# Sums and differences of the Fourier weights made earlier, by VectorE through DRAM, and two squares more per stream left to the matmul

## The chip, the cores and the metric

The kernel runs on one core of one Trainium2 chip. The metric is the device time of one execution in microseconds (us), as the median of several runs. A difference within 0.2% is one that a measurement of this kernel can hardly tell from none.

## What is computed

A block of two layers works on 256 latent tokens and 256 context tokens of 1024 features. Each layer is a half SwiGLU FFN, a token mixer and a second half SwiGLU FFN; each of the three is preceded by an RMS norm with a shift and a scale, and added to the stream through a gate. Layer 0 mixes by a two-dimensional Fourier transform in four groups of 256 features, followed by a weight matrix; layer 1 mixes by retention. Cut to what matters:

```python
def half_ffn(t, m, j):
    h = modulate(rmsnorm(t, norm_g[l, j]), m[3 * j], m[3 * j + 1])
    return t + 0.5 * m[3 * j + 2] * swiglu(h, w_gate, w_up, w_down)

def fourier_mix(h):                       # layer 0
    hg = h.reshape(b, n, 4, 256)
    f = jnp.fft.fft2(hg, axes=(1, 3), norm="ortho").real
    return f.reshape(b, n, d)

def fourier_layer(h_lat, h_ctx, w, bias):
    return fourier_mix(h_lat) @ w + bias, fourier_mix(h_ctx) @ w + bias
```

Everything is float32. The kernel makes one float32 product of three TensorE matmuls: each operand is split into a rounded part ("hi") and the rest ("lo"), and hi x hi, hi x lo and lo x hi are added up.

## The kernel before, in words

The streams lie transposed, features on partitions, as eight tiles of 128 features by 256 tokens for each of the two streams (xlat, xctx). Weights come from DRAM in blocks of 1 MB by the SP queue into three buffers (`raw`, `rpool`), are split by ScalarE (`wh`, line 88, a cast) and VectorE (`wl`, line 89, a subtraction) into a ring of five buffers for each of the two parts (`wpool`, 1024 columns each), and are read by TensorE (`mm3`, lines 126 to 128). The order in which each engine's instructions stand is set by a scheduler that simulates the program; `tc.issue_after` holds an instruction back behind another.

The first FFN walks over 22 blocks of gate and up weights in three chunks (`half_ffn`, loop over i), each chunk followed by four blocks of the down projection (b). Beside it VectorE makes the modulation vectors by row products (`ada_step`, line 216, called by `pump`), whose weights POOL loads (line 207). The last chunk's down projection ends in `project_last`: for each of the eight tiles d and both streams s VectorE adds the residual (line 363), `scale_parts` makes the scaled hi and lo parts that the Fourier stage reads (lines 341 and 342), and `square` squares the tile (ScalarE, line 265) and adds the square to the running sum (POOL, line 272). With `apart=True` the square of the last tile, d = 7, is not added but kept as a second tile in `sums[s]`, and the matmul that sums over features adds it (`start` and `stop` over the list).

The Fourier stage (`fourier`) goes thus:

- `wide_tails` (lines 485 to 488) splits the weights of four lone frequencies and the bias.
- `stage1` transforms along features, for three (stream, group) pairs ahead; then `rstd_tokens` (line 352) makes the sums over features of the squares, one column for each half stream, and from them the reciprocal root (lines 357 and 359).
- For each pair `fold` (lines 587 to 591) applies the root and adds and subtracts halves, splits the result (`t` of line 89), and `stage2` transforms along tokens. In the trace these tiles are the `t` of the matmuls ps<-a,t.
- Then the weight matrix: four blocks b of two output tiles, each a product over odd and even frequencies, with residual (line 363), square and add (line 272; stream 0 on VectorE, stream 1 on POOL). Block 0 is loaded in `project_last` ahead of its last block (`fourier_weights`), blocks 1 to 3 inside the stage.

The weights of a frequency and of its mirror are needed as sum and difference. `load_folded` loads both matrices of a block (two loads of 1 MB) and POOL adds and subtracts them in place (line 107, two instructions of 128 x 1024 a block), so four blocks take eight loads in the three `raw` buffers and eight POOL instructions. After the last block `prepare(0, 2, T2)` makes the norm for the second FFN (lines 300 to 316 for the latent stream), whose first two weight blocks are split by POOL (`begin_two`, line 89 on POOL).

## Time and profile before

| | us |
|---|---|
| median of 3 runs (1679.35 to 1683.1) | 1680.78 |
| the profiled execution | 1683.79 |
| its span, first to last instruction | 1682.0 |
| TensorE busy in the span | 1637.4 (97%) |
| VectorE busy | 1142.1 (68%) |
| ScalarE busy | 627.6 (37%) |
| POOL busy | 174.9 (10%) |

The span is cut by the stages: the start to about 50 us, the first FFN to 397 us, the Fourier stage to about 463 us, and then the second, third and fourth FFN with the retention layer before the last. All times in the text are from the start of the span. A time behind a matmul in the timelines is its modelled duration; the distance between two starts says what it costs. The clock column gives the granted TensorE clock: 1.00 is 2.4 GHz, 0.50 is 1.2 GHz, and a value between them is a stretch with some time at either.

### The profile page before, as it was taken

What the parts mean: (1) busy time and instruction counts of PE and PEld (TensorE: products, weight loads), DVE (VectorE), ACT (ScalarE), POOL (GpSimd) and SP (SyncE); (2) the same over time, 40 slices, a digit from 0 to 9 for tenths busy, and PEclk for the clock granted to TensorE, in tenths of its full rate; (3) what the DMA queues carried; (4) which work ended last, traced back from release to release, by engine and by line L of the source; (5) the groups of instructions that cost most, each with busy time, mean ns of one, the idle gap of its engine ahead of it and who ended that gap; (6) DMA issues with size and microseconds to landing.
All of it is one profiled execution on the core that took longest, in us unless ns stands there. A gap on an engine that the chain in (4) does not pass through costs nothing.

```text
span 1682.0 us, 23132 instructions
## 1 busy us (share of the span) xinstructions
PE 1637.4 (97%) x9320; PEld 1431.1 (85%) x9320; DVE 1142.1 (68%) x1760; ACT 627.6 (37%) x913; POOL 174.9 (10%) x211
## 2 busy tenths in 40 slices
PE   6999999998899999999999999999999999999998
PEld 4788888887898888888888888888998989999998
DVE  5678788777966766766566776743677757575554
ACT  4422322244552223233342222233464454454444
POOL 0010011035310000000400000000400000110000
PEclk9999999999899999999999999999999999999999
DMA  9555555543324444444334444522233324345452
GB/s 328 211 189 200 194 178 217 191 170 138 120 87 155 168 172 163 177 170 166 116 121 166 161 166 160 188 95 92 77 124 126 126 101 150 128 166 180 167 195 70
DMA packets 53403, 263.63 MB, mean 157 GB/s; under 512 B 6832, under 2 KB 8240, under 8 KB 35120
## 3 DMA queue, kind: packets, MB, share of 16 engines
q1 hardware_dynamic: 34176, 193.47, 32.4%
q0 software_dynamic: 18576, 68.17, 11.7%
q8 instruction: 73, 1.20, 0.3%
q10 hardware_dynamic: 544, 0.52, 0.1%
q14 instruction: 34, 0.28, 0.1%
HBM read 261.08 MB, written 1.05 MB: 156 GB/s over the span
## 4 chain that ended last, share of the span: by engine, by line
PE 88%; DVE 6%; DMA 2%; ACT 1%; issue 1%; POOL 1%; SPq 0%; DVEq 0%; POOLq 0%; ACTq 0%
PE ps L127 29%; PE ps L128 29%; PE ps L126 29%; DMA raw<-in_wgu 1%; DVE wl L89 1%; DVE q L330 1%; DVE h L332 1%; ACT wh L88 1%; DMA a<-in_ada_first 1%; DVE xctx L363 1%; DVE xlat L363 1%; DMA q<-q 0%; PE ps L818 0%; DMA xctx<-in_x 0%; PE aux L244 0%
## 5 line engine op out<-in xcount | busy, mean ns | idle before, releaser
L88 ACT CAST wh<-raw 128x1024 fp32r<-128x1024 f32 x344 | 352.9, 1030 | 710.3 <-PE ps L127 659.7
L127 PE MATMUL ps<-h,wh 128*128 128x512 f32 (+1 forms) x1600 | 563.7, 354 | 5.2 <-DVE h L332 5.1
L128 PE MATMUL ps<-h,wl 128*128 128x512 f32 (+1 forms) x1600 | 562.2, 354 | 0.0
L126 PE MATMUL ps<-h,wh 128*128 128x512 f32 (+1 forms) x1600 | 556.9, 355 | 3.2 <-ACT h L88 2.2
L89 DVE TENSOR_TENSOR wl<-raw,wh 128x1024 fp32r<-128x1024 f32 x328 | 392.7, 1200 | 168.0 <-ACT wh L88 158.6
L127 PEld LDWEIGHTS ps<-h,wh 128*128 128x128 f32 x1600 | 303.0, 190 | 48.1 <-DVE h L332 6.6
L126 PEld LDWEIGHTS ps<-h,wh 128*128 128x128 f32 x1600 | 299.5, 190 | 45.8 <-ACT h L88 3.0
L128 PEld LDWEIGHTS ps<-h,wl 128*128 128x128 f32 x1600 | 303.0, 190 | 41.2
L216 DVE CUSTOM_DVE_ANT_0 dump<-araw,wide,adab 128x1024 bf16<-128x1024 f32 x256 | 329.6, 1288 | 4.3 <-DMA araw<-in_ada_w 0.5
L128 PE MATMUL ps<-a,wl 128*128 128x512 f32 (+2 forms) x952 | 320.1, 338 | 2.5 <-DVE wl L89 2.5
L127 PE MATMUL ps<-a,wh 128*128 128x512 f32 (+2 forms) x952 | 320.3, 338 | 0.0
L126 PE MATMUL ps<-a,wh 128*128 128x512 f32 (+2 forms) x952 | 318.8, 338 | 0.2 <-ACT wh L88 0.2
L128 PEld LDWEIGHTS ps<-a,wl 128*128 128x128 f32 x952 | 182.3, 192 | 21.4 <-DVE wl L89 2.9
L127 PEld LDWEIGHTS ps<-a,wh 128*128 128x128 f32 x952 | 182.3, 192 | 18.6
L126 PEld LDWEIGHTS ps<-a,wh 128*128 128x128 f32 x952 | 181.4, 192 | 19.0 <-ACT wh L88 0.4
L430 DVE TENSOR_TENSOR t<-ps,t 128x512 f32<-128x512 f32 (+1 forms) x88 | 55.0, 625 | 188.4 <-PE ps L128 181.1
L207 POOL DMA_DIRECT2D araw<-in_ada_w x128 | 67.7, 529 | 811.3 <-DVE mods L216 742.9
L363 DVE SCALAR_TENSOR_TENSOR xlat<-ps,mods,xlat 128x256 f32<-128x256 f32 x128 | 61.1, 481 | 63.8 <-PE ps L128 63.1
L428 ACT ACTIVATE t<-ps 128x512 f32<-128x512 f32 (+1 forms) x88 | 47.9, 544 | 133.6 <-PE ps L128 133.6
L89 DVE TENSOR_TENSOR a<-t,a 128x512 fp32r<-128x512 f32 (+2 forms) x116 | 71.1, 617 | 3.9 <-ACT a L88 3.6
L89 POOL TENSOR_TENSOR wl<-raw,wh 128x1024 fp32r<-128x1024 f32 x16 | 40.0, 2516 | 282.9 <-ACT wh L88 281.0
L88 ACT CAST a<-t 128x512 fp32r<-128x512 f32 (+2 forms) x116 | 64.2, 557 | 9.2 <-DVE t L847 7.4
(208 smaller groups left out, 1201.8 us busy)
## 6 DMA issues: line engine op xcount, KB each, us to landing
raw<-in_wgu SPq DMA_DIRECT2D x85, 1024.0 KB, 4.9
araw<-in_ada_w POOLq DMA_DIRECT2D x128, 512.0 KB, 3.7
raw<-in_wd SPq DMA_DIRECT2D x32, 896.0 KB, 5.5
raw<-in_ret_in SPq DMA_DIRECT2D x24, 1024.0 KB, 4.8
raw<-in_wd SPq DMA_DIRECT2D x16, 1024.0 KB, 6.7
a<-in_ada_first SPq DMA_DIRECT2D x32, 256.0 KB, 5.1
raw<-in_four_w SPq DMA_DIRECT2D x8, 1024.0 KB, 4.9
raw<-in_ret_out SPq DMA_DIRECT2D x8, 1024.0 KB, 4.7
```

Source lines behind the costliest of these rows:

```text
L88: mark[6] = nc.scalar.copy(hi, src)
L89: i = (lo_eng or nc.vector).tensor_tensor(lo, src, f32(hi), ALU.subtract)
L126: nc.tensor.matmul(ps, lh, rh, start=start, stop=False)
L127: nc.tensor.matmul(ps, lh, rl, start=False, stop=False)
L128: mark[4] = nc.tensor.matmul(ps, ll, rh, start=False, stop=stop)
L207: nc.gpsimd.dma_start(raw, a["ada_w"][l, m, d])
L216: nc.vector.tensor_tensor_reduce(dump, raw, wide[:, v, :], 1.0, adab[:, l, m, d : d + 1], ALU.mult, ALU.add, mods[l][:, m, d, v : v + 1],)
L330: nc.vector.scalar_tensor_tensor(u, x_tile(d, s), sc, r, ALU.mult, ALU.mult)
L332: done.append(nc.vector.scalar_tensor_tensor(lo, u, sh, f32(hi), ALU.add, ALU.subtract))
L363: mark[0] = nc.vector.scalar_tensor_tensor(x_tile(d, s), ps, mods[l][:, m, d, s : s + 1], x_tile(d, s), ALU.mult, ALU.add)
L428: mark[1] = nc.scalar.activation(sg[:, :width], psg[:, :width], AF.Silu)
L430: nc.vector.tensor_tensor(hf[:, :width], psu[:, :width], sg[:, :width], ALU.mult)
```

## The change

- `load_folded` is gone. `fold_step` loads a quarter of the two matrices' pair (two loads of 512 KB, 128 x 1024), VectorE adds and subtracts in place (two instructions of 128 x 512), and SP stores the result in a DRAM tile `folded`. There are eight such steps, one after every second gate and up block of the first FFN (i odd, from 3 to 17), each held behind the block's last split. Its buffers take 12 KB of a partition; the space for the DMA descriptors of the POOL queue is cut to 4 KB for them (last line of the diff).
- The four Fourier weight blocks are then single loads of 1 MB from `folded`, split as any other block.
- `wide_tails` is called with block 0, ahead of the last down projection block.
- `square(apart=...)` takes a count. At the end of the first FFN it is 2: the squares of d = 6 and d = 7 are left to the matmul of `rstd_tokens`, which has three parts instead of two. Elsewhere it is 0 or 1 as before.

```diff
+    fpool = ctx.enter_context(tc.tile_pool(name="fpool", bufs=1))
+    dpool = ctx.enter_context(tc.tile_pool(name="dpool", bufs=1, space=bass.MemoryType.DRAM))
...
-    def load_folded(src, other, n):
-
-        raw, two = load_raw(src, n), load_raw(other, n)
+    folded = dpool.tile([4, P, 2048], F32, name="folded")
+    folds = [(b, o) for b in range(4) for o in (0, 1024)]
+
+    def fold_step(slot):
+
+        b, o = folds.pop(0)
+        raw, two = (fpool.tile([P, WT], F32, tag=f"f{i}", bufs=2 - i, name=nm("fold")) for i in range(2))
+        for i, t in enumerate((raw, two)):
+            nc.sync.dma_start(t, a["four_w"][slot, b, i][:, o : o + WT])
         for i, op in enumerate((ALU.add, ALU.subtract)):
             u, v = (t.rearrange("p (g f c) -> p g f c", f=2, c=256)[:, :, i] for t in (raw, two))
-            nc.gpsimd.tensor_tensor(u, u, v, op)
-        return raw
+            nc.vector.tensor_tensor(u, u, v, op)
+        nc.sync.dma_start(folded[b][:, o : o + WT], raw)
...
-    def square(d, s, eng=nc.gpsimd, apart=False):
+    def square(d, s, eng=nc.gpsimd, apart=0):
...
-        elif apart and d == ND - 1:
+        elif d >= ND - apart:
             sums[s].append(sq)
...
-                        start=(i == 0), stop=(i == 1),
+                        start=(i == 0), stop=(i == len(sums[s]) - 1),
...
                 if b == 3:
-                    fourier_weights(l // 2)
+                    fourier_weights()
...
-                        square(d, s, apart=True)
+                        square(d, s, apart=2)
...
                 hidden(*pss)
+                if f == 0 and folds and i % 2:
+                    with tc.issue_after(mark[0].ins):
+                        fold_step(0)
                 pump(RATE[f])
...
-    def fourier_weights(slot):
-        four["blk"] = wparts(four_load(slot, 0), 2048)
+    def fourier_weights():
+        four["blk"] = wblock(folded[0], 2048)
+        four["wt"] = wide_tails(0)
...
-        wt = wide_tails(slot)
+        wt = four["wt"]
...
         for b in range(4):
-            if b == 0:
-                blk, ready = four["blk"], four_load(slot, 1)
-            else:
+            blk = four["blk"]
+            if b:
                 with tc.issue_after(four["last"][0].ins), tc.issue_after(four["last"][1].ins):
-                    blk = wparts(ready, 2048)
-                if b < 3:
-                    ready = four_load(slot, b + 1)
+                    blk = wblock(folded[b], 2048)
...
-    nc = bacc.Bacc("TRN2", target_bir_lowering=False, num_devices=1)
+    nc = bacc.Bacc("TRN2", target_bir_lowering=False, num_devices=1, dynamic_dma_scratch_size=4096)
```

The scheduler moves the DMAs and some instructions with it. Three places follow, each as it stood and as it stands now (line numbers are those of the two versions: 95 of before is 97 now, 107 is 115, 272 is 280, 89 is 91, 488 is 499).

SP's queue at the start, from the late half of the first gate and up block to the first whole block (raw_759 before, raw_765 now). Before:

```order
L95 DMA raw_289<-in_wgu 128x1024
L1043 DMA fing<-in_final_g 128x8
L711 DMA lg<-in_decay 128x8
L95 DMA raw_295<-in_wgu 128x1024
L95 DMA raw_301<-in_wgu 128x1024
L95 DMA raw_759<-in_wgu 128x2048
```

Now:

```order
L97 DMA raw_295<-in_wgu 128x1024
L1049 DMA fing<-in_final_g 128x8
L112 DMA fold_833<-in_four_w 128x1024
L112 DMA fold_834<-in_four_w 128x1024
L112 DMA fold_1000<-in_four_w 128x1024
L717 DMA lg<-in_decay 128x8
L97 DMA raw_301<-in_wgu 128x1024
L97 DMA raw_307<-in_wgu 128x1024
L97 DMA raw_765<-in_wgu 128x2048
```

Three loads of Fourier weights, 1.5 MB, stand ahead of the decay values and of the late halves of the second and third block.

SP's queue in the first FFN's first chunk, at the first two stores, now:

```order
L97 DMA raw_1187<-in_wd 128x2048
L116 DMA folded<-fold_833 128x1024
L112 DMA fold_1001<-in_four_w 128x1024
L112 DMA fold_1168<-in_four_w 128x1024
L97 DMA raw_1263<-in_wd 128x2048
L97 DMA raw_1339<-in_wd 128x2048
L116 DMA folded<-fold_1000 128x1024
L112 DMA fold_1169<-in_four_w 128x1024
```

Before, the down projection's loads followed each other there. Each store is now followed at once by the second load of the next step, without a weight load between them.

POOL from the first square of the last down projection to the squares of the Fourier stage. Before:

```order
L272 TENSOR_TENSOR q_3173<-q_3137,q_3171 128x256
L272 TENSOR_TENSOR q_3180<-q_3144,q_3178 128x256
L107 TENSOR_TENSOR raw_3622<-raw_3622,raw_3624 128x4x256 x2
L488 TENSOR_TENSOR a_3290<-raw_3287,t_3296 32x512
L272 TENSOR_TENSOR q_3233<-q_3173,q_3231 128x256
L272 TENSOR_TENSOR q_3240<-q_3180,q_3238 128x256
L107 TENSOR_TENSOR raw_3718<-raw_3718,raw_3720 128x4x256 x2
L107 TENSOR_TENSOR raw_3818<-raw_3818,raw_3820 128x4x256 x2
L272 TENSOR_TENSOR q_3708<-q_3665,q_3706 128x256
L272 TENSOR_TENSOR q_3765<-q_3708,q_3763 128x256
L89 TENSOR_TENSOR wl_4089<-raw_4086,wh_4088 128x1024
L89 TENSOR_TENSOR wl_4093<-raw_4086,wh_4092 128x1024
```

Now:

```order
L280 TENSOR_TENSOR q_3235<-q_3199,q_3233 128x256
L280 TENSOR_TENSOR q_3242<-q_3206,q_3240 128x256
L499 TENSOR_TENSOR a_3267<-raw_3264,t_3273 32x512
L91 TENSOR_TENSOR wl_4135<-raw_4132,wh_4134 128x1024
L280 TENSOR_TENSOR q_3760<-q_3717,q_3758 128x256
L280 TENSOR_TENSOR q_3813<-q_3760,q_3811 128x256
L91 TENSOR_TENSOR wl_4139<-raw_4132,wh_4138 128x1024
```

The first two rows of each are the squares of d = 5. The sums and differences and the adds of d = 6 are gone between them and the next stage, and the two weight splits for the second FFN stay (one of them ahead of two adds).

## Rows read from the trace of the kernel before

**Rows 1.** The page's first line and its list of busy time, share of the span and instructions.

```profile
span 1682.0 us, 23132 instructions
PE 1637.4 (97%) x9320; PEld 1431.1 (85%) x9320; DVE 1142.1 (68%) x1760; ACT 627.6 (37%) x913; POOL 174.9 (10%) x211
```

**Rows 2.** Busy time by stretch: start and end in us, its length, then busy us and (instructions) of PE, PEld, DVE, ACT and POOL, the granted clock, the DMA engines' share and GB/s. The first row lies in the first FFN, the others in the Fourier stage.

```profile
250.00:300.00 50.00, 50.00 (x222) 41.38 (x222) 42.77 (x66) 12.27 (x14) 5.28 (x10) 1.00 0.62 222
400.00:405.00 5.00, 2.46 (x12) 2.46 (x12) 0.56 (x1) 0.00 (x0) 3.01 (x4) 0.72 0.64 226
420.00:430.00 10.00, 8.10 (x49) 7.27 (x49) 7.52 (x31) 5.72 (x23) 0.00 (x0) 0.83 0.01 2
440.00:460.00 20.00, 16.31 (x105) 15.52 (x105) 19.90 (x30) 8.98 (x19) 13.31 (x8) 0.84 0.28 99
```

**Rows 3.** Timeline of PE in the Fourier stage: start us, duration us, engine, line, operation, out<-in, shapes, and in brackets the idle time ahead and what ended it.

```profile
397.22 0.28 PE L126 MATMUL ps<-a,h 128*128 128x256 f32 x1
402.54 3.57 PE L352 MATMUL aux<-meanw,q 128*128 128x1 f32 x16 [5.04 <-POOL q L272]
405.97 0.56 PE L127 MATMUL ps<-a,h 128*128 128x256 f32 x1
...
413.91 0.39 PE L128 MATMUL ps<-a,t 128*128 128x256 f32 x1 [1.07 <-DVE t L89]
...
423.35 0.39 PE L126 MATMUL ps<-a,t 128*128 128x256 f32 x1 [0.71 <-ACT t L88]
...
424.65 0.39 PE L128 MATMUL ps<-a,t 128*128 128x256 f32 x1 [0.81 <-DVE t L89]
...
429.62 0.28 PE L128 MATMUL ps<-a,wl 128*128 128x258 f32 x1
...
456.64 0.43 PE L128 MATMUL ps<-a,wl 128*128 128x256 f32 x1 [2.04 <-DVE wl L89]
...
462.98 0.38 PE L300 MATMUL aux<-meanw,q 128*128 128x1 f32 x2 [1.31 <-DVE q L272]
```

**Rows 4.** Timeline of POOL in the same stage, columns as in rows 3.

```profile
392.02 1.62 POOL L272 TENSOR_TENSOR q<-q,q 128x256 f32<-128x256 f32 x2 [0.79 <-ACT q L265]
395.41 4.87 POOL L107 TENSOR_TENSOR raw<-raw,raw 128x1024 f32<-128x1024 f32 x2 [1.77 <-DMA raw<-in_four_w]
...
401.76 1.40 POOL L272 TENSOR_TENSOR q<-q,q 128x256 f32<-128x256 f32 x2
408.72 4.85 POOL L107 TENSOR_TENSOR raw<-raw,raw 128x1024 f32<-128x1024 f32 x2 [5.56 <-DMA raw<-in_four_w]
438.35 4.93 POOL L107 TENSOR_TENSOR raw<-raw,raw 128x1024 f32<-128x1024 f32 x2 [24.78 <-DMA raw<-in_four_w]
...
448.75 5.89 POOL L89 TENSOR_TENSOR wl<-raw,wh 128x1024 fp32r<-128x1024 f32 x2 [1.95 <-DVE t L669]
```

**Rows 5.** Timeline of ACT: the last square of the first FFN (q<-xctx), and the root that follows the sums.

```profile
396.76 0.40 ACT L265 ACTIVATE q<-xctx 128x256 f32<-128x256 f32 x1
406.15 0.26 ACT L357 ACTIVATE root<-aux,epst 128x4 f32<-128x4 f32 x1 [8.99 <-PE aux L352]
```

**Rows 6.** Timeline of DVE: two instructions of `fold` beside line 107 on POOL and the same two later; residuals beside it, later, and beside POOL's weight splits; and the residual of the last tile.

```profile
409.85 1.48 DVE L89 TENSOR_TENSOR a<-t,a 1x128 fp32r<-1x128 f32 x1
411.36 2.49 DVE L89 TENSOR_TENSOR t<-t,t 128x256 fp32r<-128x256 f32 x1
...
414.78 0.28 DVE L89 TENSOR_TENSOR a<-t,a 1x128 fp32r<-1x128 f32 x1
...
415.30 0.42 DVE L89 TENSOR_TENSOR t<-t,t 128x256 fp32r<-128x256 f32 x1
...
438.43 2.58 DVE L363 SCALAR_TENSOR_TENSOR xlat<-t,mods,xlat 128x256 f32<-128x256 f32 x1
440.94 2.62 DVE L363 SCALAR_TENSOR_TENSOR xctx<-t,mods,xctx 128x256 f32<-128x256 f32 x1
...
443.56 0.47 DVE L363 SCALAR_TENSOR_TENSOR xlat<-t,mods,xlat 128x256 f32<-128x256 f32 x1
...
449.80 2.59 DVE L363 SCALAR_TENSOR_TENSOR xlat<-t,mods,xlat 128x256 f32<-128x256 f32 x1
452.32 2.60 DVE L363 SCALAR_TENSOR_TENSOR xctx<-t,mods,xctx 128x256 f32<-128x256 f32 x1
...
462.84 0.95 DVE L363 SCALAR_TENSOR_TENSOR xlat<-t,mods,xlat 128x256 f32<-128x256 f32 x1
```

**Rows 7.** Groups of DVE instructions in the whole span, by shape: count, then busy us and mean ns of one, then the idle time ahead. The first is an add of two SBUF tiles of the shape that a fold step has.

```profile
L896 DVE TENSOR_TENSOR t<-t,a 128x512 f32<-128x512 f32 x8 | 5.3, 682 | 0.0
```

**Rows 8.** The start: busy time of one stretch (columns as in rows 2); ACT's casts of the late halves of the second and third weight block; and the first matmul of PE that needs the last tiles of the norm.

```profile
32.00:36.00 4.00, 4.00 (x30) 2.87 (x29) 0.97 (x2) 0.00 (x0) 0.00 (x0) 1.00 1.01 367
40.60 1.05 ACT L88 CAST wh<-raw 128x1024 fp32r<-128x1024 f32 x1 [0.26 <-DMA raw<-in_wgu]
41.88 1.05 ACT L88 CAST wh<-raw 128x1024 fp32r<-128x1024 f32 x1 [0.23 <-DMA raw<-in_wgu]
48.01 1.21 PE L126 MATMUL ps<-h,wh 128*128 128x512 f32 x4 [1.17 <-ACT h L88]
```

**Rows 9.** A DMA issue on the page: count, KB each, median us from issue to landing; and SP's longest wait at its queue in the stretch from 300 to 520 us (us in total, times, longest).

```profile
raw<-in_wgu SPq DMA_DIRECT2D x85, 1024.0 KB, 4.9
SPq L95 <- DVE wl L89: 146.2, 15, 19.8
```

More of the change, by code (lines that the diff above doesn't have):

```diff
@@ L378, in one @@
             residual(d, ps[:, :S], l, m, s)
-            square(d, s, nc.gpsimd if both else nc.vector, not both)
+            square(d, s, nc.gpsimd if both else nc.vector, int(not both))
             if each is not None:
@@ L548, in fourier_begin @@
         four.update(h=h, dcols=dcols, tails=tails, fix=fix, nyq=nyq, edge=edge, lone=lone, halves=halves)
-    def four_load(slot, b):
-        return load_folded(a["four_w"][slot, b, 0], a["four_w"][slot, b, 1], 2048)
-    def fourier_weights(slot):
-        four["blk"] = wparts(four_load(slot, 0), 2048)
+    def fourier_weights():
+        four["blk"] = wblock(folded[0], 2048)
+        four["wt"] = wide_tails(0)
     def fourier(l, slot, after):
@@ L671, in fourier @@
                     residual(d, z[:, STREAMS[s]], l, 5, s)
-                    square(d, s, nc.gpsimd if s else nc.vector, s == 0)
+                    square(d, s, nc.gpsimd if s else nc.vector, int(s == 0))
                     if d == ND - 1 and s == 0:
@@ L921, in project_out @@
                     if hd == HEADS - 1:
-                        square(d, 0, nc.vector, True)
+                        square(d, 0, nc.vector, 1)
                 if half == 0 and between is not None:
```

## The prediction

> **What bounds the kernel now.** I read the page's first lines, then who waited for whom on TensorE, then busy time by stretch, and last the timelines of all four engines around the one stretch that stood out. TensorE is busy 1637.4 of 1682.0 us [rows 1], so only the time in which it waits or runs at half clock can be won. In the first FFN it never waits, and VectorE has idle time there: 7.2 of 50 us in its fullest stretch [rows 2]. The Fourier stage is the place. At 402.54 TensorE has waited 5.04 us for POOL, the longest single wait in that stage, ahead of the sums over features [rows 3]. ACT's last square had ended at 397.16 [rows 5]. What came last was POOL's add of d = 6: it stood behind two sums and differences and a small tail split and ran from 401.76 on [rows 4]. After the wait the granted clock is 0.72 and 0.59 in the two stretches of 5 us, that is 2.8 and 4.1 us at 1.2 instead of 2.4 GHz [rows 2].
>
> The same POOL instructions do harm a second time. Beside the third pair (408.72 to 413.57) two VectorE instructions took 1.48 and 2.49 us that otherwise take 0.28 and 0.42; beside the fourth (438.35 to 443.28) two residuals took 2.58 and 2.62 us instead of 0.47 [rows 4, 6]. VectorE does not get on until POOL's instruction is over. TensorE's waits at 413.91, 423.35 and 424.65 are for the chain that VectorE and ScalarE work through in that time [rows 3]. The fourth pair also came late, after 24.78 us without data: its loads stood in line for the three buffers [rows 4]. The weights of the last block were therefore split late, and TensorE waited 2.04 us for them at 456.64 [rows 3].
>
> **The change, part by part.** The sum is made against the profiled execution's own 1683.79 us (span 1682.0 and 1.8 around it), which lies 3.0 above the median of 1680.78; I take the difference off the median.
>
> *Term A, the sums over features.* The adds of d = 6 leave POOL, and so do the sums and differences. POOL's adds of d = 5 ended at 393.64 [rows 4]; now only a tail split follows. TensorE's last matmul ahead of the sums starts at 397.22 [rows 3], the last square ends at 397.16 [rows 5]. So the sums start near 397.6 instead of 402.54 (0.3 for a square that the tail split may delay). They grow from two parts to three: 24 records in place of 16. The 16 took 3.43 us to the next matmul at 405.97, at half clock: 0.214 each [rows 3]. At full clock I take half of that, 24 x 0.107 = 2.6 us, an estimate; were it no faster, 5.1. The end moves from 405.97 to about 400.2: 5.8 us, of which I take 5.6. Bounds: 3.0 (start at 397.9, no faster records) and 6.1 (start at 397.3).
>
> *Term B, folding and transforming along tokens, 405.97 to 429.62.* These 23.65 us hold 1.07 of wait at 413.91 and 1.90 in the stretch from 420 to 430 [rows 2, 3], and two spells of half clock: 3.1 us of the first one lie behind 405.97, and 3.4 us in the later stretch (0.83 over 10 us) [rows 2]. Each such us costs half a us, 3.25 together, so that 17.4 us at full clock remain. VectorE gets back 1.20 + 2.07 = 3.27 us [rows 6]. The least gain is 1.07 + 1.55 = 2.6, if the later waits and the later spell stay; the most is 5.0, if only some 1.2 of waits are left, since the waits from 421 on are for the same chain, which then comes 3.3 earlier. I take 4.0, nearer the upper end, because each of these waits is for a split of that chain [rows 3].
>
> *Term C, the weight matrix, 429.62 to the last residual, which ends at 463.79* [rows 3, 6]. TensorE ends its product some us before VectorE ends the last residual, and the next norm waits for that one (at 462.98, [rows 3]); VectorE sets this end, busy 19.90 of 20 us [rows 2]. It gets back 2.58 + 2.62 - 0.94 = 4.26 us from the fourth pair [rows 6]. One load in place of two for a block lets the last block be split before it is needed, so the wait of 2.04 goes, which lies beside. Not gone are POOL's two weight splits for the second FFN, 5.89 us at 448.75 [rows 4], beside which two residuals also took 2.59 and 2.60 [rows 6]; they come earlier now, beside other residuals, at the same price. Least 2.0 (TensorE's wait alone), most 6.0 (4.26, and 1.7 for a spell of half clock of 3.4 us, out of the 6.4 us between 440 and 460, [rows 2]). I take 4.3.
>
> *Added on VectorE.* Sixteen adds of 128 x 512 at 0.682 us [rows 7]: 10.9 us, over the blocks from about 78 to 330 us. A block is 48 matmuls, 222 of them are in 50 us [rows 2], so a block lasts 10.8 us and a step comes every 21.6. In that time VectorE has 7.2/50 x 21.6 = 3.1 us to spare, and a step takes 1.4. Cost on the path: nothing. Without that cover it would be 10.9 at most.
>
> Here a page speaks against moving the work. The Trainium skill, "Perfetto Trace Analysis", section "Optimizing Scalar/DVE Operations", recalls that GPSIMD and DVE share an SBUF read port, and that moving operations between those two therefore might not help. By it terms B and C would be in doubt and the sum would be A alone, 5.6; by the rows it is the place that counts, since POOL in the first FFN has only 5.28 us of DMA issues in 50 [rows 2], and nothing there for VectorE to wait behind.
>
> *Added DMAs.* Eight loads of 1 MB become sixteen of half a MB, eight stores and four loads of 1 MB. In the first FFN the DMA engines are busy 0.62 of the time [rows 2] and a MB lands 4.9 us after its issue [rows 9]; one step brings 1.5 MB in 21.6 us. On SP's queue a store waits for VectorE's adds, and the weight loads stand behind it; they wait for buffers of their own 10 to 20 us long as it is [rows 9]. Nothing.
>
> *The start.* Three loads, 1.5 MB, now stand ahead of the late halves of the second and third weight block, where the DMA engines have no time left: 367 GB/s, share 1.01 [rows 8]. That makes 4.1 us. The two casts (40.60 and 41.88) could come at 44.7 and 46.0; TensorE reads them after 48.01 [rows 8]. It waited 1.17 us there for a part of the norm that had stood behind such casts on ACT, and that wait may go. Bounds: a gain of 1.2, a loss of 4.1. I take nothing.
>
> *The rest.* The tail weights' split is moved ahead on ScalarE, which is idle over half the time; the smaller space for POOL's descriptors serves two loads in flight as before. Nothing.
>
> The sum is 5.6 + 4.0 + 4.3 = 13.9: 1683.79 - 13.9 = 1669.9 for an execution like the profiled one, and 1680.78 - 13.9 = **1666.9** for the median. After the stage TensorE is full to the end, so the gain stays.
>
> **The rivals.** *POOL's remaining work fills the room.* Ten adds before the sums, eight after, and two weight splits of 2.9 us each stay on POOL; if VectorE's chain keeps waiting behind them, terms B and C go and A stays: 1680.78 - 5.6 = 1675.2. For it: beside the splits residuals were as slow as beside the sums [rows 6]. Against it: 9.8 of POOL's us in the two terms' stretches are gone. This is also what the page named above would lead one to expect.
>
> *The start slips.* The weights there come 4.1 us later and TensorE waits for them: 1666.9 + 4.1 = 1671.0. For it: full DMA engines [rows 8]. Against it: the two weight halves had over 6 us between their casts and 48.01.
>
> *Both together*: 5.6 - 4.1 = 1.5 less, 1679.3, within 0.2% (3.4 us, about what a measurement of this kernel can tell from no change).
>
> *Slower: VectorE stands still in front of a step's adds.* The second load of a step goes into a single buffer and is issued only after the step before it and its store. If it stood behind two weight loads that each wait a block for their buffer, it would land 2 x 10.8 + 4.9 = 26.5 us after, 4.9 later than the next step's turn, and everything on VectorE would queue behind the adds, the weight splits that TensorE needs among it. Less the 1.7 us to spare, that is 3.2 us a step, 22 over seven steps: 1689. It decides from 3.7 us a step on (1.7 to spare and 2.0, a seventh of 13.9). Against it: in the new order that load stands directly behind its store, with no weight load between, and lands some 15 us ahead of its turn.
>
> **How the numbers follow.** The forecast gets 0.66, the first rival 0.12, the slipped start 0.10, both together 0.06, the slower case 0.06. So faster 0.88, within 0.2% 0.06, slower 0.06. The lower end of the range is all upper bounds, 6.1 + 5.0 + 6.0 + 1.2 = 18.3: 1662.5. The upper end takes in the lower bounds (7.6: 1673.2), the slipped start and the first rival: 1676. Outside lie the last two cases.
>
> **What would show it.** In the changed kernel's profile: TensorE's wait ahead of the sums under 0.5 us, and the clock at 1.00 there (A); the folds' splits on VectorE near 0.42 us each and waits under 1.5 us in the stretch of 24 us behind the sums, now about 19.5 (B); residuals beside POOL's splits alone over 2 us, no wait of over 1 us for `wl`, and the last residual about 14 us earlier, near 450 (C); full TensorE from 50 to 397 us, with VectorE some 1 to 3 us fuller per 50. Wrong it would be with a wait for a fold load on VectorE, with TensorE's wait for `wh` or `wl` between 45 and 60 us, or with the end of the first FFN later than 397.

## The result: 12.7 us less, and the profile after

The changed kernel takes 1669.08 us (median of 4 runs, 1667.73 to 1669.94), beside 1681.76 us of the kernel before on the same chip (1679.35 to 1683.1). The ratio is 0.9925, 95% interval 0.9908 to 0.9943: faster by over three times the 0.2% that a measurement can tell from no change. The profiled execution takes 1669.94 us with a span of 1668.2, 13.8 us less than [rows 1].

The page's first line and its busy times, and the group of the new adds from the view of groups by shape between 50 and 395 us (count | busy us, mean ns | idle time ahead):

```profile
span 1668.2 us, 23165 instructions
PE 1631.1 (98%) x9328; PEld 1426.7 (86%) x9328; DVE 1137.0 (68%) x1776; ACT 626.6 (38%) x913; POOL 152.8 (9%) x201
...
L115 DVE TENSOR_TENSOR fold<-fold,fold 128x512 f32<-128x512 f32 x16 | 10.3, 685 | 0.0
```

GpSimd has 22.1 us less to do. The 16 adds cost VectorE 685 ns each (682 were taken from [rows 7]), and 0.0 us of idle time stands ahead of them: VectorE never waited for a fold load.

TensorE's timeline in the Fourier stage, as in [rows 3] (new line numbers: 352 is 360, 126 to 128 are 134 to 136, 300 is 308, 89 is 91):

```profile
396.05 0.28 PE L136 MATMUL ps<-a,h 128*128 128x256 f32 x1
396.17 2.74 PE L360 MATMUL aux<-meanw,q 128*128 128x1 f32 x24
398.77 0.47 PE L134 MATMUL ps<-a,h 128*128 128x256 f32 x1
...
412.81 0.39 PE L136 MATMUL ps<-a,t 128*128 128x256 f32 x1 [0.27 <-DVE t L91]
...
414.40 0.38 PE L134 MATMUL ps<-a,t 128*128 128x256 f32 x1 [0.72 <-ACT t L90]
...
415.70 0.40 PE L136 MATMUL ps<-a,t 128*128 128x256 f32 x1 [0.80 <-DVE t L91]
...
420.29 0.28 PE L665 MATMUL ps<-a,a 96*128 96x258 f32 x1
...
448.54 0.38 PE L308 MATMUL aux<-meanw,q 128*128 128x1 f32 x2 [3.83 <-DVE q L280]
```

The wait of 5.04 us ahead of the sums is gone: they follow the matmul at 396.05 directly, and the next one comes 2.60 us after their start (24 x 0.108). ScalarE's last square, as in [rows 5], now ends 2 us ahead of them:

```profile
393.70 0.40 ACT L273 ACTIVATE q<-xctx 128x256 f32<-128x256 f32 x1
398.95 0.26 ACT L365 ACTIVATE root<-aux,epst 128x4 f32<-128x4 f32 x1 [4.84 <-PE aux L360]
```

All waits for `wl` are gone too. The wait behind the product, for VectorE's residuals and the add behind them, has grown from 1.31 us [rows 3] to 3.83. VectorE's and then GpSimd's rows there, as in [rows 6] and [rows 4]:

```profile
401.30 0.43 DVE L91 TENSOR_TENSOR t<-t,t 128x256 fp32r<-128x256 f32 x1
...
433.30 2.63 DVE L371 SCALAR_TENSOR_TENSOR xlat<-t,mods,xlat 128x256 f32<-128x256 f32 x1
435.85 0.96 DVE L371 SCALAR_TENSOR_TENSOR xctx<-t,mods,xctx 128x256 f32<-128x256 f32 x1
...
438.36 2.62 DVE L371 SCALAR_TENSOR_TENSOR xctx<-t,mods,xctx 128x256 f32<-128x256 f32 x1
...
448.59 0.76 DVE L371 SCALAR_TENSOR_TENSOR xlat<-t,mods,xlat 128x256 f32<-128x256 f32 x1
```

```profile
432.71 2.94 POOL L91 TENSOR_TENSOR wl<-raw,wh 128x1024 fp32r<-128x1024 f32 x1 [42.91 <-ACT wh L90]
...
438.28 2.41 POOL L91 TENSOR_TENSOR wl<-raw,wh 128x1024 fp32r<-128x1024 f32 x1
```

A fold's split takes 0.43 us and not 2.49. The residuals that still take 2.6 us stand beside the two weight splits that are left on GpSimd.

Busy time by stretch (columns as in [rows 2]): the fullest stretch of the first FFN, then from the end of the sums to the first matmul of the tail weights (L665), and from there to the end of the last residual; behind it the latter two of the kernel before:

```profile
250.00:300.00 50.00, 50.00 (x223) 41.40 (x221) 44.08 (x67) 12.67 (x14) 5.28 (x10) 1.00 0.66 241
398.77:420.29 21.52, 19.73 (x135) 19.12 (x135) 16.80 (x65) 12.68 (x44) 0.00 (x0) 0.84 0.00 1
420.29:449.35 29.06, 25.03 (x209) 24.75 (x207) 27.82 (x54) 15.90 (x32) 10.48 (x8) 1.00 0.40 145
```

```profile
405.97:429.03 23.06, 19.96 (x131) 18.62 (x132) 19.91 (x65) 12.66 (x43) 4.85 (x2) 0.87 0.20 76
429.03:463.79 34.76, 29.56 (x210) 28.49 (x209) 32.45 (x54) 16.14 (x32) 16.49 (x10) 0.89 0.40 152
```

In the second stretch VectorE has 3.1 us less to do, but the length falls by 1.5 only: the clock is 0.84 there, lower than before. In the third VectorE has 4.6 us less and the clock is at 1.00; the length falls by 5.7.

Up to the end of the third stretch the clock is at half (0.50, that is 1.2 GHz) in three spells of some 3.4 us each, one of them at the start of the first FFN, where the kernel before has none. A stretch of 2 us in each, same columns:

```profile
24.00:26.00 2.00, 2.00 (x21) 1.44 (x21) 1.27 (x6) 1.04 (x1) 0.00 (x0) 0.50 1.02 399
400.00:402.00 2.00, 2.00 (x11) 2.00 (x11) 1.94 (x8) 1.33 (x4) 0.00 (x0) 0.50 0.00 0
416.00:418.00 2.00, 2.00 (x11) 2.00 (x11) 1.85 (x8) 0.72 (x3) 0.00 (x0) 0.50 0.00 0
```

### The profile page after: what moved, and what is told of

Read it like the earlier page. It is cut to its first block, busy times and chain, and to the rows that moved or that the text cites. A ratio compares the mean times of both kernels' runs of the same rounds, so it can differ in the third digit from the quotient of the medians.

```text
span 1668.2 us, 23165 instructions
## 1 busy us (share of the span) xinstructions
PE 1631.1 (98%) x9328; PEld 1426.7 (86%) x9328; DVE 1137.0 (68%) x1776; ACT 626.6 (38%) x913; POOL 152.8 (9%) x201
## 4 chain that ended last, share of the span: by engine, by line
PE 94%; DVE 3%; DMA 1%; ACT 1%; issue 0%; SPq 0%; DVEq 0%; ACTq 0%
PE ps L135 31%; PE ps L136 31%; PE ps L134 31%; DVE q L338 1%; DVE h L340 1%; DMA a<-in_ada_first 1%; PE ps L824 0%; DVE xctx L371 0%; ACT wh L90 0%; DMA xctx<-in_x 0%; PE aux L197 0%; PE aux L252 0%; DVE q L299 0%; PE aux L910 0%; DVE a L91 0%
```

## Experiments

Times are medians of this kernel's runs, ratios with their 95% interval against the kernel before on the same chip (1681.0 to 1682.5 us). The four columns of lengths come from TensorE's and VectorE's timelines of the profiled execution: the first FFN from its first product to the last 512-column matmul; A from there to the first matmul behind the sums; B to the first matmul of the tail weights; C to the end of the last residual of `xlat`. One execution of each kernel was profiled, so differences of the size of one spell of half clock (1.7 us for 3.4 us of it) need not belong to the kernel. The first FFN has such a spell in changed, presplit and apart3 (near 24 us) and in fold_pool (from 127.6 us), and in no other row.

| Kernel | us | ratio | first FFN | A | B | C |
|---|---|---|---|---|---|---|
| before | 1681.76 | 1 | 369.04 | 13.29 | 23.06 | 34.76 |
| changed | 1669.08 | 0.9925 (0.9908 to 0.9943) | 368.39 | 7.14 | 21.52 | 29.06 |
| apart1 | 1667.39 | 0.9912 (0.9899 to 0.9926) | 367.69 | 6.25 | 19.95 | 29.28 |
| apart2_only | 1677.16 | 0.9968 (0.9956 to 0.9981) | 368.58 | 7.14 | 23.57 | 34.40 |
| fold_pool | 1673.90 | 0.9953 (0.9940 to 0.9967) | 373.04 | 7.14 | 19.98 | 29.11 |
| fold_dve_late | 1674.64 | 0.9954 (0.9941 to 0.9966) | 368.81 | 6.25 | 24.25 | 31.15 |
| hold_start | 1669.95 | 0.9935 (0.9922 to 0.9947) | 367.41 | 7.14 | 20.32 | 29.06 |
| add4 | 1668.42 | 0.9925 (0.9913 to 0.9938) | 366.90 | 7.13 | 21.56 | 29.07 |
| ffn2_dve | 1667.16 | 0.9913 (0.9899 to 0.9926) | 367.27 | 7.45 | 21.50 | 26.20 |
| presplit | 1665.97 | 0.9908 (0.9895 to 0.9922) | 368.42 | 7.14 | 21.54 | 26.24 |
| before_scratch | 1681.30 | 0.9997 (0.9988 to 1.0007) | 369.03 | 13.36 | 23.10 | 34.75 |
| presplit_apart1 | 1661.64 | 0.9874 (0.9859 to 0.9889) | 366.86 | 6.25 | 18.53 | 26.50 |
| presplit_all | 1659.82 | 0.9869 (0.9853 to 0.9885) | 367.03 | 6.24 | 18.53 | 25.36 |
| apart3 | 1668.61 | 0.9919 (0.9905 to 0.9932) | 368.38 | 8.85 | 20.46 | 29.10 |

### Which part of the change brings term A

**apart1**: the squares' part undone.

```diff
-                        square(d, s, apart=2)
+                        square(d, s, apart=1)
```

> The changed kernel with the squares' part undone: in the first FFN the adds of d = 6 are on GpSimd again and the sums have two parts, 16 one-column matmuls. Theory 1 (what counted is that the sums and differences no longer stand ahead of these adds on GpSimd): GpSimd is free from 389.8 us on, two adds of 0.8 us are done well before the sums start at 396.17, so nothing is lost and 8 one-column matmuls of 0.107 us are saved: 1668.2 to 1669.1 us, TensorE's wait ahead of the sums 0. Theory 2 (the squares' part is what brought term A): the wait of some 5 us ahead of the sums comes back and the time is 1669.1 + 5.6 = 1674.7.

1667.39 us: nothing is lost. GpSimd's adds of d = 6 and TensorE's sums:

```profile
390.04 1.68 POOL L280 TENSOR_TENSOR q<-q,q 128x256 f32<-128x256 f32 x2
...
395.76 1.84 PE L360 MATMUL aux<-meanw,q 128*128 128x1 f32 x16
```

The adds end at 391.7, 4 us ahead of the sums, which take 1.84 us in place of 2.74. Theory 1 holds. With the folds gone from the stage, the squares' part of the change only lengthens A, by 0.89 us; by the intervals alone the two kernels cannot be told apart.

**apart2_only**: the squares' part alone, on the kernel before (its diff is that of the change in `square`, `rstd_tokens` and the call, and nothing of the folds).

> The kernel before with the squares' part alone: the adds of d = 6 are left to the matmul, the sums and differences stay on GpSimd at their old place. Theory 1 (either part frees the sums of GpSimd, so term A comes whole, and terms B and C do not): 1681.8 - 5.6 = 1676.2 us, last residual about 6 us earlier than 463.79, two VectorE instructions beside each of the last two pairs still at 1.5 to 2.6 us. Theory 2 (the sums start earlier but the third pair, which comes when its loads land, then meets VectorE at another place and takes the gain back): 1680 to 1682.

1677.16 us, 4.5 less than before on the same chip where 5.6 was expected. A is the whole 6.15 us shorter, B and C are not. The sums, and then VectorE's long rows beside the last two pairs of GpSimd's sums and differences:

```profile
396.05 2.74 PE L352 MATMUL aux<-meanw,q 128*128 128x1 f32 x24
...
408.63 1.93 DVE L89 TENSOR_TENSOR a<-t,a 1x128 fp32r<-1x128 f32 x1
...
410.80 2.24 DVE L89 TENSOR_TENSOR t<-t,t 128x256 fp32r<-128x256 f32 x1
...
431.54 2.62 DVE L363 SCALAR_TENSOR_TENSOR xctx<-t,mods,xctx 128x256 f32<-128x256 f32 x1
434.15 2.55 DVE L363 SCALAR_TENSOR_TENSOR xlat<-t,mods,xlat 128x256 f32<-128x256 f32 x1
```

So either part of the change brings A, and of the two only the folds' leaving GpSimd in the stage brings B and C.

### Place or engine

**fold_pool**: the new place, the old engine.

```diff
-            nc.vector.tensor_tensor(u, u, v, op)
+            nc.gpsimd.tensor_tensor(u, u, v, op)
```

> The changed kernel with its 16 adds on GpSimd instead of VectorE, still in the first FFN and through DRAM. Theory 1 (the place counts, and so does the engine once VectorE has little to spare): the Fourier stage is as in the changed kernel, but a pair of 4.9 us on GpSimd costs VectorE up to 4.3 us of standing behind it, with some 3.1 us to spare a step, so up to 1.2 x 8 = 9.6 us may be lost in the first FFN: 1669 to 1679 us, VectorE instructions of 2.4 us and more beside the adds. Theory 2 (the place alone counts): 1669.1 within 1 us, first FFN full and no longer. Theory 3 (the engine alone counts): the gain is gone, 1681.

1673.90 us, 4.8 more than the change; the intervals touch at their ends, and the profiles tell the two apart. The stage is no longer than in the changed kernel; the first FFN is, in one place. Rows of GpSimd, then VectorE, then TensorE there:

```profile
104.78 3.61 POOL L115 TENSOR_TENSOR fold<-fold,fold 128x512 f32<-128x512 f32 x2 [8.11 <-DMA fold<-in_four_w]
108.34 0.57 POOL L215 DMA_DIRECT2D araw<-in_ada_w  x1
...
118.41 4.27 POOL L115 TENSOR_TENSOR fold<-fold,fold 128x512 f32<-128x512 f32 x2 [6.77 <-DMA fold<-in_four_w]
```

```profile
116.70 1.29 DVE L224 CUSTOM_DVE_ANT_0 dump<-araw,wide,adab 128x1024 bf16<-128x1024 f32 x1 [3.55 <-DMA araw<-in_ada_w]
...
119.24 2.30 DVE L91 TENSOR_TENSOR wl<-raw,wh 128x1024 fp32r<-128x1024 f32 x1
121.47 2.30 DVE L224 CUSTOM_DVE_ANT_0 dump<-araw,wide,adab 128x1024 bf16<-128x1024 f32 x1
```

```profile
126.41 0.50 PE L134 MATMUL ps<-a,wh 128*128 128x512 f32 x1 [3.99 <-ACT a L90]
```

Two things add up. The issue of a modulation load (108.34) stood behind the two adds on GpSimd, which had themselves waited 8.11 us for a fold load: it comes 3.3 us after VectorE has done with the load's buffer (105.00), in the changed kernel 0.3 us (107.09 after 106.79). VectorE then waited 3.55 us for its data (1.80 us at the like place of the changed kernel); then two of VectorE's instructions took 2.30 us beside GpSimd's adds in place of 1.22 and 1.28. TensorE waited 3.99 us, its only wait in the first FFN, and a spell of half clock follows at 127.6 us. The loss lies in theory 1's range, but it comes from one event, not from 1.2 us in each of eight steps, and a part of it from a mechanism that I had not written down.

**fold_dve_late**: the old place, the new engine, on the kernel before.

```diff
-            nc.gpsimd.tensor_tensor(u, u, v, op)
+            nc.vector.tensor_tensor(u, u, v, op)
```

> The kernel before with its sums and differences on VectorE at their old place, in the Fourier stage: eight adds of 128 x 1024 of about 1.25 us. Theory 1 (it is GpSimd's instructions that harm, by the place of the adds of d = 6 behind them and by VectorE's standing still): term A comes, some 5 us, and in the stage VectorE spends 5.0 us on two pairs where it lost 3.3 + 4.3 = 7.5 before: 1681.8 - 5 - 2.5 = 1674 us. Theory 2 (only the work's leaving the stage counts): 1680 to 1682.

1674.64 us where theory 1 said 1674: the change of engine alone gives over half of what the change gives. A pair on VectorE:

```profile
400.08 2.36 DVE L107 TENSOR_TENSOR raw<-raw,raw 128x1024 f32<-128x1024 f32 x2 [3.03 <-DMA raw<-in_four_w]
...
432.49 2.35 DVE L107 TENSOR_TENSOR raw<-raw,raw 128x1024 f32<-128x1024 f32 x2
```

A pair takes 2.36 us there and 4.87 on GpSimd [rows 4]. A comes whole, C comes by 3.6 us, but B is 1.2 us longer: the pair at 400.08 stands ahead of the folds, and TensorE waits 2.55 us for ScalarE's `t` at 404.17. The new place with the old engine (fold_pool, 7.7 us) and the new engine at the old place (7.0) each give over half of the change's 12.7. They overlap in term A, which both have whole. The 7.7 is not the place's alone: fold_pool also has the squares' part and the single loads of a block.

### Is the cover in the first FFN real

**add4**: four more adds in each fold step.

```diff
             nc.vector.tensor_tensor(u, u, v, op)
+            for _ in range(2):
+                nc.vector.tensor_tensor(v, u, v, ALU.add)
```

> The changed kernel with four more adds of 128 x 512 in each of its eight fold steps (into a tile that is not used again): a step takes 6 x 0.684 = 4.1 us of VectorE and not 1.4. Theory 1 (the adds are hidden since VectorE has about 3.1 us to spare in two blocks): the excess of 1.0 us a step shows in steps that follow at two blocks' distance, at most 8 x 1.0 = 8 us and less where a phase of the down product lies between: 1670 to 1677, waits of TensorE in the first FFN. Theory 2 (VectorE's share is no limit there at all, and the 3.1 us were read too low): 1669.1, TensorE full from 50 to 395 us. Theory 3 (the adds are not hidden even as they are): over 1669.1 + 16 = 1685.

The view of groups by shape and the busy times from 50 to 395 us:

```profile
L117 DVE TENSOR_TENSOR fold<-fold,fold 128x512 f32<-128x512 f32 x32 | 21.2, 686 | 0.0
```

```profile
50.00:395.00 345.00, 345.00 (x1544) 285.76 (x1542) 294.41 (x450) 114.59 (x163) 44.63 (x68) 1.00 0.62 220
```

21.2 us more on VectorE, and TensorE is full throughout: 1668.42 us. Theory 2 holds: 3.1 us to spare in two blocks was too low a figure. It was read in the fullest 50 us. Over the whole 345 us VectorE is busy 272.2 us in the kernel before, which leaves 72.8, and eight steps with six adds each need 33; in which blocks it catches up was not looked at. The adds of the change are hidden with room to spare.

### The start

**hold_start**: the loads of the first two fold steps held back.

```diff
         for i, t in enumerate((raw, two)):
+            if len(folds) >= 6:
+                nc.vector.memset(t[:, 0:1], 0.0)
             nc.sync.dma_start(t, a["four_w"][slot, b, i][:, o : o + WT])
```

> The changed kernel with the loads of its first two fold steps held back by a memset of one column on VectorE, so that they are issued in the block of the step and not ahead of the late weight halves at the start. Theory 1 (the three early loads pushed the two weight halves back, their casts then stood behind ScalarE's parts of the norm, and TensorE's wait of 1.17 us at 48 us went for that reason): the casts come near 40.6 and 41.9 again, the wait comes back, the first FFN ends 1.2 us later, 1669.1 + 1.2 = 1670.3. Theory 2 (the start is shorter for another reason): 1669.1, no wait there. Theory 3 (the slower case of the prediction): a step's adds are reached before the late loads land, VectorE stands still some us, and TensorE waits for weight splits between 60 and 120 us: over 1672.

ScalarE's casts of the two late weight halves stand ahead of its parts of the norm again, as in [rows 8]:

```profile
38.73 1.05 ACT L90 CAST wh<-raw 128x1024 fp32r<-128x1024 f32 x1 [0.66 <-DMA raw<-in_wgu]
40.02 1.05 ACT L90 CAST wh<-raw 128x1024 fp32r<-128x1024 f32 x1 [0.23 <-DMA raw<-in_wgu]
```

Yet TensorE does not wait at 48 us, and the first FFN is 1.6 us shorter than before; counted from the first product, these casts come 1.3 us earlier than before. VectorE waits once for a fold load, 0.64 us at 83.30, and TensorE not at all. Theory 3 falls, and theory 1 with it: in the kernel before, the casts end at 42.93, and ScalarE then stands idle until its part of the norm gets VectorE's `mods`:

```profile
45.27 1.09 ACT L1025 ACTIVATE t<-t,mods 128x256 f32<-128x256 f32 x2 [2.33 <-DVE mods L197]
```

This part comes 21.6 us after the first product before, 20.0 in hold_start and 19.4 in the changed kernel. **before_scratch** tried the one other thing that the changed kernel and hold_start have in common at the start:

```diff
-    nc = bacc.Bacc("TRN2", target_bir_lowering=False, num_devices=1)
+    nc = bacc.Bacc("TRN2", target_bir_lowering=False, num_devices=1, dynamic_dma_scratch_size=4096)
```

> The kernel before with nothing but the smaller space for GpSimd's DMA descriptors (dynamic_dma_scratch_size=4096); every engine's order is the same. Theory 1 (the first FFN of the changed kernel is 0.7 to 2.1 us shorter because of this space, since it is so with the fold loads early and with them held back): 1681 - 1.4 = 1679.6 us, TensorE's wait at 48 us gone, the first FFN some 1.4 us shorter from TensorE's first product on. Theory 2 (the space costs and gives nothing, as the prediction has it): 1681 within 1 us and the wait there.

0.9997 (0.9988 to 1.0007): nothing, and the wait is there:

```profile
47.73 1.67 PE L126 MATMUL ps<-h,wh 128*128 128x512 f32 x6 [1.32 <-ACT h L88]
```

Theory 2 holds. The first FFN is up to 2 us shorter in kernels that fold ahead on VectorE. The wait of 1.0 to 1.4 us that is gone is a part of it, and the spell of half clock takes 1.7 back where it stands; why VectorE's `mods` come earlier, and the rest, stay open.

### What sets the end of term C

**ffn2_dve**: the remaining splits off GpSimd.

```diff
-        blks, banks = [load(0, nc.gpsimd)], [(bank(), bank()) for _ in range(2)]
+        blks, banks = [load(0)], [(bank(), bank()) for _ in range(2)]
...
-            blks.append(load(1, nc.gpsimd))
+            blks.append(load(1))
```

> The changed kernel with the weight splits that open the second and third FFN on VectorE instead of GpSimd. Theory 1 (beside GpSimd's two splits at 432.7 and 438.3 VectorE's residuals of 2.63, 0.96, 0.63 and 2.62 us lose 4.9 us against 0.48 each, and VectorE sets the end of the stage): two splits of 1.22 us cost less than that, the last residual comes 4.9 - 2.4 = 2.5 us earlier, TensorE's wait of 3.83 us ahead of the next sums falls to some 1.3, and the time is 1666.6, less what the two later splits take from the norm (up to 2.4 us, so 1666.6 to 1669). Theory 2 (the rival of the prediction that GpSimd's remaining work does not matter): VectorE only gets 2.4 to 4.9 us more to do, 1671 to 1674.

C is 2.9 us shorter, 2.5 were expected, and TensorE's wait for the residuals falls from 3.83 to 2.94 us. The whole time (1667.16) falls by less, and by the intervals it cannot be told from the changed kernel's.

**presplit**: a fold step splits as well, and both parts are loaded straight into the operand tiles.

```diff
-        nc.sync.dma_start(folded[b][:, o : o + WT], raw)
+        nc.scalar.copy(two.bitcast(F32R), raw)
+        nc.vector.tensor_tensor(raw.bitcast(F32R), raw, two, ALU.subtract)
+        for i, t in enumerate((two, raw)):
+            nc.sync.dma_start(folded[b, i][:, o : o + WT], t)
...
+    def split_block(b):
+        pairs = []
+        for o in (0, WT):
+            pair = []
+            for i, n in enumerate(("wh", "wl")):
+                t = wpool.tile([P, WT], F32R, tag=n, name=nm(n))
+                nc.sync.dma_start(f32(t), folded[b, i][:, o : o + WT])
+                pair.append(t)
+            pairs.append(tuple(pair))
+        return pairs
...
-                with tc.issue_after(four["last"][0].ins), tc.issue_after(four["last"][1].ins):
-                    blk = wblock(folded[b], 2048)
+                blk = split_block(b)
```

> The changed kernel, in which a fold step also splits its sums into the two parts that the matmuls use and both parts go to DRAM; the Fourier stage loads them straight into the operand tiles. Eight casts of ScalarE and eight subtractions of VectorE (1.22 us each, 9.8 us) leave the stage and enter the first FFN; the loads are twice the bytes. Theory 1 (VectorE sets the end of the weight-matrix part, 27.8 of 29.1 us busy, TensorE waits 3.83 us for it there, and in the first FFN a step of 2.6 us still fits into 3.1): that wait goes and the last residual comes about 3.8 us earlier: 1665.3. Theory 2 (the loads, which now need the operand tiles themselves and not a staging buffer, come too late for TensorE): waits of TensorE for wh or wl behind a DMA, of some us for each of the last three blocks, 1669 to 1680. Theory 3 (the first FFN has no room for 2.6 us a step): TensorE waits before 395 us, 1669 or more.

```profile
420.80:447.04 26.24, 25.02 (x209) 24.75 (x207) 20.82 (x48) 10.54 (x26) 9.35 (x8) 1.00 0.48 161
```

C is 2.8 us shorter, not 3.8: VectorE is busy 20.82 of 26.24 us and no longer the bound, TensorE with 25.02 is. No wait for a load shows, and the first FFN is full. Theory 1, by the smaller size: 1665.97 us (0.9908); its interval overlaps with the changed kernel's.

**presplit_apart1** and **presplit_all** put the edits together (the latter with that of ffn2_dve too).

> The fold steps split ahead of the stage, and the squares' part undone: both edits add up if each is what it seems. Theory 1: against the kernel before 15.0 us from the first and 1.2 to 1.7 us more from the second (eight one-column matmuls less, and the clock not at half behind them): 1681 - 16.5 = 1664.5. Theory 2 (the half-clock spell behind the sums comes and goes with its moment in the stage, not with the sums): 1666 within 1.

> As the run with the split ahead and the squares' part undone, and the weight splits that open the second and third FFN on VectorE too. Theory 1 (VectorE now has room in the stage, and GpSimd's splits still hold up two residuals by 2.1 us each and ScalarE's squares behind them): 0.5 to 2 us faster than that run, 1663. Theory 2 (after the split ahead TensorE sets the end of the stage, so VectorE's residuals no longer count, and four splits of 1.22 us stand ahead of the norm on VectorE): equal or up to 2.4 us slower, 1664.5 to 1667.

The busy times of B and C in presplit_apart1:

```profile
396.40:414.93 18.53, 16.70 (x133) 15.88 (x133) 16.65 (x65) 12.53 (x43) 0.00 (x0) 1.00 0.11 46
414.93:441.43 26.50, 25.29 (x211) 25.01 (x209) 20.83 (x48) 10.62 (x26) 9.35 (x8) 1.00 0.47 159
```

1661.64 and 1659.82 us, 21 to 23 less than before and better than both kernels of this case; the two cannot be told apart. It is more than theory 1's 1664.5. In the stage that is the clock, which stays at 1.00 all through: VectorE has as much to do in B as in presplit (16.65 and 16.78 us), and B takes 18.53 us in place of 21.54. But outside the stage too the profiled execution of presplit_apart1 is shorter than that of presplit, by 1.6 us in the first FFN (the spell of half clock there) and 2.5 behind the last residual. It is the fastest of its kernel's four, at a mean clock of 0.999; the others have 0.996 to 0.998.

**apart3**: the squares of three tiles left to the matmul.

> The changed kernel with the squares of the last three tiles left to the matmul: four parts, 32 one-column matmuls ahead of the stage. Theory 1 (each further part costs its 8 one-column matmuls, 0.86 us, and the longer such a stretch, the likelier the clock is at half for 3.4 us behind it, which is 1.7 us): 1669.1 + 0.9 = 1670.0 where the clock falls as it does in the changed kernel, the sums 3.6 us long, the clock at 0.5 just behind them. Theory 2 (the half-clock spell has nothing to do with the sums; where they stand alone counts): 1670.0 too if it falls, but 1668.3 with the clock at 1.00 behind the sums. Theory 3 (a part costs nothing, since TensorE would wait there for something else): 1669.1.

```profile
397.02 4.44 PE L360 MATMUL aux<-meanw,q 128*128 128x1 f32 x32
```

A is 1.7 us longer than the change's: 0.86 for eight more one-column matmuls at 0.108, and the rest because the clock falls during the sums. The whole time (0.9919) does not show it. The runs do not tell theories 1 and 2 apart. The clock went to half behind the sums in five kernels with 24 or 32 one-column matmuls (changed, add4, ffn2_dve, presplit, apart3), not in three others with 24 (hold_start, fold_pool, apart2_only), nor in the four with 16 and no wait at the sums (apart1, fold_dve_late, presplit_apart1, presplit_all). With one profiled execution of each, that does not settle whether the sums have to do with it.

## Why the prediction was right, point by point

The gain was forecast as 13.9 us and is 13.8 between the two profiled executions, 12.7 between the medians. The miss (1666.9 for 1669.1) is 1.2 us of gain too much; the other 1.0 is the kernel before, whose median over all runs lies 1.0 above the one that I started from. That the sum came out so near is partly luck: against the forecast A gave 0.5 us more, C 1.4 more and the start 1.0 that was put at nothing, while B gave 2.5 less and 0.6 was given back behind the stage. The mechanism was right in A and C, and in B the size was not.

**Term A: right.** 5.6 forecast, 6.15 measured (13.29 to 7.14): the sums wait for nothing, 2.6 us for 24 one-column matmuls was 2.60, and apart1 and apart2_only show that the order on GpSimd's queue was the cause. One statement in it was wrong: that the clock would be at 1.00 there. It held during the sums, and then it was at half from 398.9 to 402.4 although TensorE had not waited.

**Term B: the mechanism right, the size wrong.** 4.0 forecast, bounds 2.6 to 5.0; between the same two matmuls it is 1.8 (429.62 answers to 420.65), 1.5 by the table. VectorE got its 3.1 us back, and the waits fell from 3.10 to 1.79, a little over the 1.5 that I had set. The step that failed is that the spell of half clock would leave with the wait. At a mean clock of 0.84 the 21.52 us hold some 6.9 us at half clock, which cost 3.4 us; before it was 0.87, 6.0 us. Where the clock stays up (presplit_apart1), B is 18.53 us, 4.5 less than before, between the forecast and its upper end. With one spell it is 19.95 to 20.32 (apart1, fold_pool, hold_start).

**Term C: right, a little more.** 4.3 forecast, bounds 2.0 to 6.0; 5.5 measured by the same matmuls, 5.7 by the table. VectorE sets the end, as was said, and got 4.6 us back. TensorE's waits for `wl` are gone, and so are the spells (clock 1.00 in place of 0.89), the part that I had kept for the upper bound. That the single loads were needed for this is not shown: fold_dve_late has two loads a block, and no wait for `wl` either. The two splits on GpSimd stayed at the same price, 2.6 us for a residual.

**The adds and the loads: nothing, right.** add4 shows that even three times the work is hidden.

**The start: nothing forecast, 1.0 gained.** TensorE's last matmul of 512 columns comes at 391.63 us in place of 392.68. The wait at 48 us went, which stood in the bound, and a spell of half clock came that nobody had forecast. The two casts came at 44.11 and 46.57 us, near the 44.7 and 46.0 of the prediction; that the wait would go because they moved is refuted by hold_start.

**The rivals.** GpSimd's remaining work costs C 2.9 us (ffn2_dve); it did not fill the room. The slipped start and the standing still before a step's adds did not come: in the changed kernel no fold load is waited for. The rule of the Trainium skill in "Perfetto Trace Analysis", section "Optimizing Scalar/DVE Operations", that moving work between GPSIMD and DVE might not help, did not decide here: with the place unchanged, the change of engine alone gave 7.0 us (0.9954). The sharing that it gives as the reason fits the rows: in fold_pool VectorE's instructions took 2.30 us beside GpSimd's adds.

After the last residual the gain was 14.4 us, in the span it is 13.8; 0.6 is given back behind 1192 us, and I have not traced it.

## What to carry to other kernels

Before work is moved, split a cost into what it holds up by its place in its own queue, what it does to the engine beside it, and what the other engine pays for it. Here the first was 6.15 us (A), the second 3.1 and 4.6 us of VectorE's time (B and C), and the third nothing at the place chosen, and experiments told them apart. Do not count half-clock time as gone with the wait that stood ahead of it: take one estimate with it and one without, and do not read a difference of the size of one such spell as the kernel's from one profile each. When an engine has proven room, ask what else can leave the crowded stage with the first piece: splitting the weights ahead, and leaving out the part that had become needless, gave another 7 us.

## What the hardware showed that I had not expected

- TensorE's clock went from 2.4 to 1.2 GHz without any wait of TensorE's ahead of it: behind 24 one-column matmuls (2.6 us) in the changed kernel, and already during 32 in apart3. With the split ahead and the shorter sums together no such spell is left in the stage: the clock is 1.00 from 395 to 460 us and 0.999 over the whole span of the profiled execution of presplit_apart1, against 0.991 before.
- GpSimd's queue issues DMAs as well as it computes. Behind two adds of 3.61 us in all an issue came 3.3 us after its buffer was free; VectorE waited 3.55 us for the data, which landed 8.3 us after the issue, and TensorE 3.99 us in the end.
- A small wait at the start (1.0 to 1.4 us at 47 to 48 us) is there in the four kernels that fold in the Fourier stage and in none of the ten that fold ahead, whether the early loads come early or late.
